# An output projection by seven block products (Strassen) instead of eight, in a hybrid decoder block

## Chip, cores, metric

The kernel runs on one core of a Trainium2 chip. The metric is the device time of one execution in microseconds (us). All arithmetic is float32: a product of two float32 matrices is made of three TensorE matmuls, since each operand is held as a rounded high part and a low remainder (hi·hi, lo·hi and hi·lo, summed in one PSUM bank).

## What is computed

One decoder block over 1024 tokens of width 1024: two branches (a state-space branch and a forgetting-attention branch, "fox") are gated and summed, and one projection takes the sum back into the residual stream. Cross-attention to 256 memory tokens and a gated feed-forward follow.

```python
D_MODEL = 1024; SEQ = 1024
out_a = glu_a * jax.nn.sigmoid(glu_b)            # state-space branch
out_b = att @ w_fox_o[l]                          # forgetting attention
gate_a, gate_b = jnp.split(jax.nn.sigmoid(gate_logits), 2, axis=-1)
h = h + (gate_a * out_a + gate_b * out_b) @ w_mix_out[l]      # <- the projection
h = h + memory_cross_attention(rms_norm(h, norm_mem_q[l]), ...)
f_a, f_b = jnp.split(rms_norm(h, norm_ffn[l]) @ w_ffn_in[l], 2, axis=-1)
h = h + (jax.nn.silu(f_a) * f_b) @ w_ffn_out[l]
```

## The kernel before

The kernel is written in stages. Within a stage a scheduler orders the instructions of each engine; each engine then runs its list in that order, and so do the queues of transfers (nearly all loads and stores are issued by SyncE, called SP; some stores by ScalarE). The part that the change touches is `stage_tail` and one place in the attention stage.

`fox_part(j)` makes rows 128j to 128j+127 of the gated sum, transposed (channels on partitions, tokens along the row), in two halves of 512 tokens: 12 matmuls for each half, times a gate that is loaded (`gb`), added to `sg`. The result is split at once into `mxh` (ScalarE cast) and `mxl` (VectorE subtraction) and stays in SBUF as `mT`. There are eight such parts, each 24 matmuls.

`mix(t, c, wm)` then makes 128 tokens times 512 output channels: eight blocks of 128 channels, three matmuls each, so 24 matmuls of 128x512 into one bank; a VectorE add puts the bank and a loaded piece of x (`xr`) into `H[t]`. Eight token tiles by two halves make 16 groups, 384 matmuls. The weights are loaded and split on chip (`whi`/`wlo` for c=0, `wbh`/`wbl` for c=1).

Two kinds of work are woven between those groups. `ahead(j)` splits the first feed-forward weights (`wpr` into `wph`, `wpl`) and stores them to `w_d`, by transfers that ScalarE issues. `norm(t)` normalises a finished tile for the memory attention: two squares on ScalarE (L190), small VectorE operations and a power on GpSimd (L207 to L217), one VectorE scaling into the single buffer `xs` (L231), eight TensorE transposes into two banks (L237), and a split into `u2h`, `u2l` (L183, L184). Tiles 0 to 3 are normalised behind groups 13 to 16 of the projection:

```python
    for t in range(4, NT):
        mix(t, 1, wm1)
        norm(t - 4, gq, u2)
```

`mem_q`, which follows, needs the normalised tiles 0 to 3 for its first matmul group. Much earlier, at the start of the attention stage, `Fox.run` copies the weights of the gated unit into `wg_d` by SP transfers, and then stores cumulated log-gates to `cum_d` (`cch`, `cl`) and loads them back as `hb`, which the first row-maximum matmul of the attention (L1763) reads.

Of the kernel before, what the change touches and what calls it, by code (L numbers as in the profile page):

```python
# [9 lines left out]
F32 = mybir.dt.float32  # L10
# [108 lines left out]
class Block:  # L119
# [125 lines left out]

    def norm_turn(self, xs, act, t):

        for b in range(2):
            cast = self.turned(self.turn(xs, b, ("misc", "pv")[b]), b, act, t)
        return cast  # L250
# [59 lines left out]
def hybrid_block_kernel(ctx: ExitStack, tc: tile.TileContext, x, mem, norm_mix, w_in, b_forget,  # L310
# [29 lines left out]
    sh = Shared(ctx.enter_context(tc.tile_pool(name="sh", bufs=1, reuse_waits="tile")))  # L340
    wg_d = B.dram.tile([4, P, 2 * D], F32, name="wg_d")
    glu = Glu(B, sh, yT, wg_d, gate_d)
    with tc.tile_pool(name="fox", bufs=1, reuse_waits="tile") as fp:
        fox = Fox(B, fp, sh, uT, w_in, b_forget[0], cum_d, rd_d, att_d)
        fox.run(y_d, yT, aT, w_glu, wg_d, [f for j in range(4) for f in glu.values(j)])
    glu.after = fox.maxima[NH - 2]
    with tc.tile_pool(name="st2", bufs=1, reuse_waits="tile") as s2:
        stage_tail(B, big, s2, sh, x, glu, aT, gate_d, kv_d, w_fox_o, w_mix_out, norm_mem_q[0], w_mem_q,
                   w_mem_o, norm_ffn[0], w_ffn_in, w_ffn_out, norm_final, out)
# [231 lines left out]

def stage_tail(B, big, s2, sh, x, glu, aT, gate_d, kv_d, w_fox_o, w_mix_out, g_mq, w_mem_q, w_mem_o, g_ffn,
               w_ffn_in, w_ffn_out, g_fin, out):
# [16 lines left out]

    mT = Act(s2, "t", NS2, 8, L, name="mx")
    fox = {}

    def fox_part(j):
# [6 lines left out]
        for h in range(2):  # L611
            cs = slice(512 * h, 512 * h + 512)
            po = B.bank(("pv", "pv", "misc")[(2 * j + h) % 3])
            B.gemm_t(po, fh[:, :, o:o + P], fl[:, :, o:o + P], aT, h, 4)
            gb = load(gate_d[D + j * P:D + (j + 1) * P, cs], "gb")
            V.tensor_mul(gb, gb, po)
            V.tensor_add(sg[:, cs], sg[:, cs], gb)
            mh, ml = mT.rhs(j, h)
            merged.append(B.split(mh, ml, sg[:, cs]))

    merged = []
    for j in range(8):
# [5 lines left out]
        if j > 2:  # L628
            fox_part(j - 3)
    for j in range(5, 8):  # L630
        fox_part(j)


    H = [bslot(name=f"h{t}") for t in range(NT)]
    gq = B.bcast_gain(s2, g_mq)
    u2 = Act(s2, "t", NS2, 8, L, name="u2")

# [4 lines left out]

    def wslots(src, pool_lo):

        nk = src.shape[0] // P
        raw = B.wpool.tile([P, RAW], F32, tag="raw", bufs=4, name="raw")[:, :D]
        S.dma_start(raw.rearrange("p (k c) -> p k c", k=nk), src.rearrange("(k p) c -> p k c", p=P))
        hl = bslot(F32R, "wbh"), bslot(F32R, "wbl")
        B.split(*hl, raw, pool_lo)
        return [t_.rearrange("p (k c) -> p k c", k=nk) for t_ in hl]  # L650

    def mix_weights(c):

        wm = ([], [])
        for kk in range(4):
            if c == 0:
                hl = B.wblock(w_mix_out, 2 * kk, 2, 0, 512)
            else:
                hl = wslots(w_mix_out[2 * kk * P:(2 * kk + 2) * P, 512:D], False)
            for w_, t_ in zip(wm, hl):  # L660
                w_ += [t_[:, 0, :], t_[:, 1, :]]
        return wm

    def mix(t, c, wm):
        cs = slice(512 * c, 512 * c + 512)
        ps = B.bank()
        gemm_n(ps, mT, t, wm, 8)
        V.tensor_add(H[t][:, cs], ps, load(x[t * P:(t + 1) * P, cs], "xr"))

    def norm(t, gb, act):  # L670
        xs = s2.tile([P, D], F32, tag="xs", bufs=1, name="xs")
        B.norm_scale(xs, H[t], B.rstd(H[t]), gb)
        return B.norm_turn(xs, act, t)

# [5 lines left out]
    def ahead(j):  # L680
# [14 lines left out]
        def plain():  # L695
            hl, _ = pair(0)
            with B.behind(merged[-1]):
                B.split(*hl, pre[j][0])
            for i, t_ in enumerate(hl):
                keep(i, t_)  # L700
# [34 lines left out]

    wm0 = mix_weights(0)
    with B.behind(merged[-1]):
        wm1 = mix_weights(1)
    mixes = [lambda t=t: mix(t, 0, wm0) for t in range(NT)] + [lambda t=t: mix(t, 1, wm1) for t in range(4)]
    weave(mixes, [f for j in range(AHEAD_IN + 1) for f in ahead(j)], 4)  # L740
    for t in range(4, NT):
        mix(t, 1, wm1)
        norm(t - 4, gq, u2)


    qT = Act(big, "big", 16, 4, L, name="mq")
# [260 lines left out]
    t_d = B.dram.tile([8, NP, P, 512], F32, name="t_d")  # L1007
    gs = {}

# [568 lines left out]
class Fox:  # L1578
# [279 lines left out]

    def run(self, y_d, yT, aT, w_glu, w_d, filler):
        B, fp, S = self.B, self.fp, self.B.S  # L1860
# [28 lines left out]
        with B.tc.issue_after(loaded.ins):  # L1889
            for k in range(4):  # L1890
                S.dma_start(w_d[k].rearrange("(m g) c -> m g c", g=8),
                            w_glu[k * P:(k + 1) * P].rearrange("(g m) c -> m g c", m=16))
        for f in pro[0].parts[:8] + pro[0].evac[:1] + pro[0].parts[8:] + pro[0].evac[1:]:
            f()
# [96 lines left out]
```

## Time and profile before

| | |
|---|---|
| three runs | 1541.27, 1540.81, 1539.42 us (median 1540.81) |
| span of the profiled execution | 1538.1 us (its own time outside the profiler isn't listed beside it) |
| TensorE (PE) busy | 1520.7 us, 99% |
| VectorE (DVE) busy | 1005.7 us, 65% |
| ScalarE (ACT) busy | 658.1 us, 43% |
| GpSimd (POOL) busy | 253.6 us, 16% |
| moved by transfers | 234.06 MB, mean 152 GB/s |

"Busy" is the time in which an engine has an instruction running; matmuls overlap, so their spacing, not their listed length, is what one costs. The median of the runs lies 2.7 us above the span. Times inside the span are counted from its start; the last part of the attention output and the projection lie between about 640 and 770 us.

### The profile page before, as it was taken

The page shows a single profiled execution, that of the slowest core. Times are in us where ns is not written, and L with a number is a line of the kernel's source. Part 1 is how long each engine was busy: PE and PEld are TensorE (multiplying, and loading weights), DVE is VectorE, ACT ScalarE, POOL GpSimd, SP SyncE. Part 2 cuts the span into 40 slices and gives each one's busy share as a digit, 9 for nine tenths or more (in the row PEclk, how much of TensorE's full clock was granted, in tenths as well). Part 3 has the DMA queues.
Part 4 walks back from the last instruction along what each step waited for, and adds up shares of the span by engine and source line. Part 5 has one row for each costly group of instructions (what it writes and reads, how often), then busy time and mean ns, then how long its engine had stood idle before and what let it go on. Part 6 is the DMA issues. An engine that isn't in the chain of part 4 may idle for free. (4 is left out here: it accounts for less than half of the span.)

```text
span 1538.1 us, 20434 instructions
## 1 busy us (share of the span) xinstructions
PE 1520.7 (99%) x7329; PEld 1257.7 (82%) x7329; DVE 1005.7 (65%) x1828; ACT 658.1 (43%) x1183; POOL 253.6 (16%) x341
## 2 busy tenths in 40 slices
PE   8999999999999999999999999999999999999998
PEld 7888888898777678888888888888888888888886
DVE  7936554355878867675556797777777775675555
ACT  7423334324667643232435663333333333354343
POOL 1166542100121214100102200000000000101001
PEclk9999999999999999999999999999999999999999
DMA  9634556611223746378210356555544544896542
GB/s 286 161 104 102 131 128 144 180 41 16 50 46 88 192 131 198 111 218 308 89 69 1 117 204 210 162 161 160 158 158 157 157 145 139 291 391 220 192 163 110
DMA packets 196293, 234.06 MB, mean 152 GB/s; under 512 B 35576, under 2 KB 127656, under 8 KB 195680
## 3 DMA queue, kind: packets, MB, share of 16 engines
q1 hardware_dynamic: 188704, 214.93, 47.0%
q10 hardware_dynamic: 7488, 17.83, 3.1%
q8 instruction: 57, 0.93, 0.3%
q14 instruction: 44, 0.36, 0.1%
HBM read 161.94 MB, written 72.71 MB: 153 GB/s over the span
## 5 line engine op out<-in xcount | busy, mean ns | idle before, releaser
L184 DVE TENSOR_TENSOR wlo<-raw,whi 128x1024 fp32r<-128x1024 f32 (+2 forms) x120 | 126.3, 1058 | 45.4 <-ACT whi L183 44.2
L183 ACT CAST whi<-raw 128x1024 fp32r<-128x1024 f32 (+2 forms) x120 | 108.7, 910 | 105.6 <-PE mm L174 39.1
L184 DVE TENSOR_TENSOR ol<-or,oh 128x1024 fp32r<-128x1024 f32 x73 | 90.1, 1236 | 74.0 <-ACT oh L183 71.9
L173 PE MATMUL mm<-uh,whi 128*128 128x512 f32 x344 | 136.5, 397 | 0.0
L174 PE MATMUL mm<-ul,whi 128*128 128x512 f32 x344 | 135.1, 393 | 0.0
L175 PE MATMUL mm<-uh,wlo 128*128 128x512 f32 x344 | 134.5, 391 | 0.0
L183 ACT CAST oh<-or 128x1024 fp32r<-128x1024 f32 x73 | 76.9, 1054 | 105.0 <-PE mm L1108 34.2
L997 POOL TENSOR_TENSOR g<-a,c 128x512 f32<-128x512 f32 x22 | 35.7, 1621 | 389.0 <-ACT a L996 389.0
L175 PEld LDWEIGHTS mm<-uh,wlo 128*128 128x128 f32 x344 | 64.7, 188 | 13.3 <-DVE wlo L184 0.2
L1803 POOL TENSOR_TENSOR pl<-pf,ph 128x512 fp32r<-128x512 f32 (+1 forms) x32 | 36.8, 1152 | 232.5 <-DVE ph L1802 193.3
L173 PEld LDWEIGHTS mm<-uh,whi 128*128 128x128 f32 x344 | 64.8, 188 | 11.6
L174 PEld LDWEIGHTS mm<-ul,whi 128*128 128x128 f32 x344 | 64.8, 188 | 11.0
L1800 ACT ACTIVATE pf<-sc 128x512 f32<-128x512 f32 (+1 forms) x96 | 46.4, 489 | 44.5 <-DVE sc L1796 28.3
L986 DVE SCALAR_TENSOR_TENSOR c<-c,pv 128x512 f32<-128x512 f32 x22 | 15.1, 687 | 76.5 <-ACT c L985 76.4
L211 POOL TENSOR_TENSOR r<-ms,mhalf 128x1 f32<-128x1 f32 (+1 forms) x26 | 15.7, 605 | 298.6 <-DVE ms L207 258.5
L964 PE MATMUL pv<-S3h,we 128*128 128x512 f32 x176 | 57.7, 389 | 0.0
L1806 DVE TENSOR_TENSOR pl<-pf,ph 128x512 fp32r<-128x512 f32 (+2 forms) x64 | 35.3, 553 | 10.4 <-ACT ph L1805 9.8
L1108 PE MATMUL mm<-ol,oh 128*128 128x512 f32 (+1 forms) x110 | 41.9, 381 | 0.0
L1108 PE MATMUL mm<-oh,ol 128*128 128x512 f32 (+1 forms) x110 | 41.9, 381 | 0.0
L1108 PE MATMUL mm<-oh 128*128 128x512 f32 (+1 forms) x110 | 41.9, 381 | 0.0
L173 PE MATMUL sc<-uh,whi 128*128 128x512 f32 x104 | 40.8, 392 | 0.0
L173 PE MATMUL mm<-yh,whi 128*128 128x512 f32 x104 | 40.7, 392 | 0.0
(639 smaller groups left out, 4554.2 us busy)
## 6 DMA issues: line engine op xcount, KB each, us to landing
or<-c_d SPq DMA_DIRECT2D x77, 256.0 KB
wo<-in_w_ffn_out_dram SPq DMA_DIRECT2D x22, 512.0 KB
c_d<-g SPq DMA_DIRECT2D x44, 256.0 KB
t_d<-wo SPq DMA_DIRECT2D x44, 256.0 KB
or<-t_d SPq DMA_DIRECT2D x44, 256.0 KB
rawb<-in_w_ffn_in_dram SPq DMA_DIRECT2D x20, 512.0 KB
raw<-in_w_ffn_in_dram SPq DMA_DIRECT2D x20, 512.0 KB
raw<-in_w_in_dram SPq DMA_DIRECT2D x19, 512.0 KB
```

What stands on the lines that cost most here:

```text
L173: T.matmul(ps, lh, rh, start=first, stop=False)
L174: T.matmul(ps, lh, rl, start=False, stop=False)
L175: return T.matmul(ps, ll, rh, start=False, stop=last)
L183: cast = self.A.copy(hi, src)
L184: self.rest = (self.G if pool_lo else self.V).tensor_sub(lo, src, f32(hi))
L211: self.G.tensor_tensor(out=r, in0=v, in1=self.mhalf[:, 0:n], op=ALU.pow)
L964: T.matmul(ps, l_[:, k, :], r_, start=first and k == 0 and i == 0, stop=k == 3 and i == 2, skip_group_check=True)
L997: G.tensor_mul(g[:, 512:], a1, c1)
L1108: T.matmul(ps, l_[:, gi], r_[:, c0:c1], start=k == 0 and (p == NP - LAST if own else p == 0 and n in (1, 2, 7)), stop=p == NP - 1 and k == ...
L1800: self.exp = A.activation(pf[:, off:], ps[:, off:], AF.Exp)
L1803: G.tensor_sub(pl[:, off:], pf[:, off:], f32(ph[:, off:]))
L1806: self.left = V.tensor_sub(pl[:, off:], pf[:, off:], f32(ph[:, off:]))
```

## The change

The 1024x1024x1024 product is cut into 2x2 blocks of 512 and made by seven block products of sums of blocks, numbered 1 to 7. The gated sum is no longer split and kept in SBUF: VectorE makes its sums of blocks in float32 (`merged_pair`, one for each pair of channel blocks) and SP stores them to `mc_d`, 28 pieces of 256 KB. The sums of the weight blocks are made by GpSimd (`mix_sums`, 16 additions of 128x512) and stored to `mt_d`, at the start of the attention stage, right behind the `wg_d` copies. For each of the 28 steps `m_get` loads the two operands side by side into one buffer, casts both in one ScalarE operation and makes the low parts on VectorE (left operand) and GpSimd (right operand). A step is 4 x 3 matmuls, 336 in all. `H` starts as x, loaded by transfers, and VectorE adds or subtracts a bank after each product (28 times, from PSUM). The last product but one runs tile by tile (`m_tile`), the last one, number 3, as four steps, and `norm(0)` to `norm(3)` are woven into these eight pieces, with both transposed halves in banks named "pv".

```diff
-    for j in range(5, 8):
-        fox_part(j)
...
+def mix_sums(B, w, mt_d, p):
+    w1, w2 = [B.wpool.tile([P, RAW], F32, tag="raw", bufs=4, name="wmix")[:, :D] for _ in range(2)]
+    for i, t_ in enumerate((w1, w2)):
+        B.S.dma_start(t_, w[(2 * p + i) * P:(2 * p + i + 1) * P, :])
+    b11, b12, b21, b22 = w1[:, :512], w1[:, 512:], w2[:, :512], w2[:, 512:]
+    for n, o, i in ((5, b11, b12), (7, b12, b22), (6, b22, b11), (4, b21, b22)):
+        B.G.tensor_add(o, o, i)
+        B.S.dma_start(mt_d[n, p], o)
...
+    def merged_pair(p):
+        ge, go = gs.pop(2 * p), gs.pop(2 * p + 1)
+        a21, a11, a22, a12 = ge[:, :512], ge[:, 512:], go[:, :512], go[:, 512:]
+        s24, s3 = slot(name="s24"), sh.half("s3")
+        for n, a_ in ((2, a12), (4, a22)):
+            S.dma_start(mc_d[n, p], a_)
+        V.tensor_sub(s3, a11, a21)
+        V.tensor_sub(a21, a22, a21)
...
+        for n, a_ in ((6, s24[:, :512]), (7, s3), (5, a21), (3, s24[:, 512:])):
+            S.dma_start(mc_d[n, p], a_)
...
+    MORDER = (1, 6, 7, 5, 4, 2, 3)
...
+    def m_get(m):
+        n, p = mseq[m]
+        r_ = B.wpool.tile([P, RAW], F32, tag="raw", bufs=4, name="raw")[:, :D]
+        S.dma_start(r_[:, :512], mc_d[n, p])
...
+        S.dma_start(r_[:, 512:], src)
...
+        A.copy(hl[0], r_)
+        V.tensor_sub(hl[1][:, :512], r_[:, :512], f32(hl[0][:, :512]))
+        G.tensor_sub(hl[1][:, 512:], r_[:, 512:], f32(hl[0][:, 512:]))
...
+    def m_step(m):
...
+        for i in range(4):
+            m_mm(m, i, set_[i])
+        if p == 3:
+            for i in range(4):
+                m_add(n, i, set_[i])
...
+    MAHEAD = 5
...
+    weave([lambda m=m: m_next(m) for m in range(2, 20)], [f for j in range(AHEAD_IN + 1) for f in ahead(j)], 4)
+    last = [lambda i=i: (m_tile(i), m_next(20 + i)) for i in range(4)] + [lambda m=m: m_step(m) for m in range(24, 28)]
+    weave(last, [lambda t=t: norm(t, gq, u2, ("pv", "pv")) for t in range(4)])
...
         for f in beside:
             f()
```

The order of instructions on the engines shows where this lands. Three places matter.

**The end of the projection, TensorE.** Before, the eight transposes of each of the four tiles (`xs` into misc and pv) stand between groups of 24 matmuls; this is the fourth set and what follows it:

```order
L173 MATMUL mm<-wbh,mxh_1_6008 128x512
L174 MATMUL mm<-wbl,mxh_1_6008 128x512
L175 MATMUL mm<-wbh,mxl_1_6016 128x512
L237 MATMUL misc<-ident,xs 128x128 x4
L237 MATMUL pv<-ident,xs 128x128 x4
L173 MATMUL sc<-u2h_0_6803,whi 128x512
L173 MATMUL mm<-u2h_0_6803,whi 128x512
```

Now the last rows of the projection (L693) and what follows; `moh` and `mol` are the split operands of a step:

```order
L693 MATMUL mm<-moh 128x512
L693 MATMUL mm<-mol,moh 128x512
L693 MATMUL mm<-moh,mol 128x512
L237 MATMUL pv<-ident,xs 128x128 x24
L173 MATMUL mm<-u2h_0_6722,whi 128x512
L174 MATMUL mm<-u2l_0_6730,whi 128x512
```

One set of eight transposes stands 22 matmuls ahead of the last product's end; the other three sets, 24 transposes, stand together behind the last matmul of the projection, directly before the first matmul of `mem_q`.

**The same place on VectorE.** Before, each tile's scaling stood one group of 24 matmuls behind the one before it:

```order
L668 TENSOR_TENSOR h_6798<-sc,xr 128x512
L184 TENSOR_TENSOR u2l_0_6811<-misc,u2h_0_6803 128x2x128
L231 SCALAR_TENSOR_TENSOR xs<-h_6795,r_7433,gbc 128x1024
L184 TENSOR_TENSOR u2l_0_6813<-misc,u2h_0_6805 128x2x128
L184 TENSOR_TENSOR u2l_0_6815<-pv,u2h_0_6807 128x2x128
```

Now (h_6714 to h_6721 are tiles 0 to 7; the adds L700 of h_6718 and h_6719 are those of the last product):

```order
L700 TENSOR_TENSOR h_6718<-h_6718,sc 128x512
L184 TENSOR_TENSOR u2l_0_6734<-pv,u2h_0_6726 128x2x128
L217 SCALAR_TENSOR_TENSOR r_7544<-rt_7545,r_7544 128x1
L215 TENSOR_TENSOR rt_7600<-r_7599 128x1
L700 TENSOR_TENSOR h_6719<-h_6719,sc 128x512
L231 SCALAR_TENSOR_TENSOR xs<-h_6715,r_7544,gbc 128x1024
L184 TENSOR_TENSOR u2l_0_6736<-pv,u2h_0_6728 128x2x128
L216 SCALAR_TENSOR_TENSOR rt_7600<-rt_7600,ms_7598 128x1
L700 TENSOR_TENSOR h_6720<-h_6720,mm 128x512
L217 SCALAR_TENSOR_TENSOR r_7599<-rt_7600,r_7599 128x1
L700 TENSOR_TENSOR h_6721<-h_6721,mm 128x512
```

The scaling of tile 1 stands behind the last product's second add, that of tile 2 behind its fourth, and tile 3's comes a further 16 rows later.

**SP at the start of the attention stage.** Before, nothing stands between the copies to `wg_d` and the cumulated gates:

```order
L1891 DMA wg_d<-in_w_glu_dram 128x1x2048 x3
L1663 DMA cum_d<-cch 8x1024
L1668 DMA cum_d<-cl 8x512 x2
L1701 DMA raw<-in_w_in_dram 128x8x64
L1702 DMA raw<-in_w_in_dram 128x8x64
L1741 DMA hb<-cum_d 2x1024
```

Now the transfers of `mix_sums` (24 in all) stand there; these are the last of them:

```order
L588 DMA wmix<-in_w_mix_out_dram 128x1024
L592 DMA mt_d<-wmix 128x512
L1740 DMA cum_d<-cch 8x1024
L592 DMA mt_d<-wmix 128x512 x3
L1745 DMA cum_d<-cl 8x512 x2
L1778 DMA raw<-in_w_in_dram 128x8x64
L1779 DMA raw<-in_w_in_dram 128x8x64
L1818 DMA hb<-cum_d 2x1024
```

The store of `cch` waits in SP's list for 13 of the 16 stores of weight sums, and `cl` and the loads of `hb` for all of them.

The same queue, later, where the products start. TensorE's list has three whole steps (36 matmuls) and parts 6 and 7 (48) mixed behind part 5, and then the fourth step. The left operand of that step is the first row below; its load is one of the x2:

```order
L633 DMA mc_d<-sg 128x512
L651 DMA mc_d<-s_6936 128x512
L644 DMA mc_d<-sg 128x512
L651 DMA mc_d<-sg 128x512
L670 DMA raw<-mc_d 128x512 x2
```

Between the store and the load stand three stores of `merged_pair(3)`, two of which need part 7's first half (`a22`, and `a22 - a21`).

More of the change, by code (lines that the diff above doesn't have):

```diff
@@ new lines, in m_mm, with m_add @@
+    def m_mm(m, i, ps):
+        n, p = mseq[m]
+        hi, lo = mops[m]
+        gi = slice(i * P, (i + 1) * P)
+        for k, (l_, r_) in enumerate(((hi, hi), (hi, lo), (lo, hi))):
+            T.matmul(ps, l_[:, gi], r_[:, 512:], start=k == 0 and p == 0 and n in (1, 2, 7),
+                     stop=p == 3 and k == 2, skip_group_check=True)
+    def m_add(n, i, ps):
+        t, c, op = {1: (4, 0, ALU.add), 2: (4, 0, ALU.add), 6: (0, 0, ALU.add), 7: (0, 1, ALU.subtract),
+                    5: (0, 1, ALU.subtract), 4: (0, 0, ALU.add), 3: (4, 1, ALU.subtract)}[n]
+        h = H[t + i][:, 512 * c:512 * c + 512]
+        return V.tensor_tensor(out=h, in0=h, in1=ps, op=op)
@@ L641, in gemm_n, with norm @@
             B.mm3(ps, ah, al, w[0][k], w[1][k], k == 0, k == nk - 1)
[L643 to L670, printed above, removed]
+    def norm(t, gb, act, banks=("misc", "pv")):
         xs = s2.tile([P, D], F32, tag="xs", bufs=1, name="xs")
         B.norm_scale(xs, H[t], B.rstd(H[t]), gb)
-        return B.norm_turn(xs, act, t)
+        return B.norm_turn(xs, act, t, banks)
     AHEAD_IN = 2
```

93 lines of the change are left out of this document (70 added, 23 removed).

## The prediction

> **What bounds the kernel now.** I read the page first, then TensorE's waits, then the busy time in the stretch of the projection.
>
> ```profile
> span 1538.1 us, 20434 instructions
> PE 1520.7 (99%) x7329; PEld 1257.7 (82%) x7329; DVE 1005.7 (65%) x1828; ACT 658.1 (43%) x1183; POOL 253.6 (16%) x341
> PE sc L258 <- POOL ident masks.py:199: 1.9, 1, 1.9
> PE mm L1763 <- DVE mc L1768: 1.2, 1, 1.2
> 680.00:700.00 20.00, 20.00 (x90) 16.53 (x89) 16.13 (x21) 8.74 (x12) 0.00 (x0) 1.00 0.91 283
> 700.00:720.00 20.00, 20.00 (x90) 16.57 (x89) 10.04 (x15) 4.51 (x7) 0.00 (x0) 1.00 0.79 269
> 720.00:740.00 20.00, 20.00 (x90) 16.57 (x89) 10.84 (x15) 7.92 (x13) 0.56 (x1) 1.00 0.91 328
> 1350.00:1370.00 20.00, 20.00 (x90) 16.57 (x89) 14.59 (x15) 10.49 (x11) 0.00 (x0) 1.00 1.05 393
> ```
>
> PE is busy 1520.7 of 1538.1 us. Its two longest waits of all are 1.9 and 1.2 us, and neither lies in the projection. In the rows of windows (stretch, its length, busy time and count of PE, its weight loads, DVE, ACT, POOL, then granted clock, busy share of the transfer engines, GB/s) PE is busy in the whole of the 60 us. So a matmul taken away there is worth its full spacing, and any microsecond in which PE waits is lost in full: nothing behind it has slack. The spacing comes from PE's timeline:
>
> ```profile
> 737.83 0.39 PE L174 MATMUL mm<-wbl,mxh 128*128 128x512 f32 x1
> 742.37 0.39 PE L173 MATMUL sc<-wbh,mxh 128*128 128x512 f32 x1
> ```
>
> These are 20 spacings apart: 4.54 / 20 = 0.227 us each.
>
> **Term 1, the matmuls.** 384 become 336: 48 x 0.227 = **-10.9 us**, all on PE.
>
> **Term 2, the end of the projection.** The order shows 24 transposes, those of tiles 1 to 3, behind the last product. One `xs` buffer makes the tiles a chain: scaling, transposes, cast, subtraction, next scaling. Before, the links look so:
>
> ```profile
> 734.40 1.22 DVE L184 TENSOR_TENSOR wlo<-raw,whi 128x1024 fp32r<-128x1024 f32 x1
> 735.53 0.21 DVE L207 TENSOR_SCALAR ms<-ss 128x1 f32<-128x1 f32 x1
> 736.41 0.16 DVE L215 TENSOR_TENSOR rt<-r 128x1 f32<-128x1 f32 x1 [0.67 <-POOL r L211]
> 750.30 0.39 PE L175 MATMUL mm<-wbh,mxl 128*128 128x512 f32 x1
> 750.53 0.60 PE L237 MATMUL misc<-ident,xs 128*128 128x128 f32 x4
> 750.73 0.69 DVE L668 TENSOR_TENSOR h<-mm,xr 128x512 f32<-128x512 f32 x1 [2.48 <-PE mm L175]
> 750.97 0.60 PE L237 MATMUL pv<-ident,xs 128*128 128x128 f32 x4
> 751.17 0.37 ACT L183 CAST u2h<-misc 128x256 fp32r<-128x256 f32 x1 [3.62 <-PE misc L237]
> 751.32 0.48 PE L173 MATMUL sc<-wbh,mxh 128*128 128x512 f32 x1
> 751.52 0.63 ACT L190 ACTIVATE junk<-h 128x512 bf16<-128x512 f32 x1
> 751.57 0.42 DVE L184 TENSOR_TENSOR u2l<-misc,u2h 128x256 fp32r<-128x256 f32 x1
> 751.91 1.28 DVE L231 SCALAR_TENSOR_TENSOR xs<-h,r,gbc 128x1024 f32<-128x1024 f32 x1
> 752.15 0.35 ACT L183 CAST u2h<-misc 128x256 fp32r<-128x256 f32 x1
> 752.40 0.63 ACT L190 ACTIVATE junk<-h 128x512 bf16<-128x512 f32 x1
> 770.63 0.19 PEld L173 LDWEIGHTS sc<-u2h,whi 128*128 128x128 f32 x1 [0.26 <-ACT u2h L183]
> ```
>
> A set of transposes takes 750.53 to 751.32 = 0.79 us. Before, PE ran a group of 24 matmuls (5.4 us) behind each set, which hid the chain; only 0.26 us was waited ahead of `mem_q` (last row). I follow the changed order of DVE and ACT with these durations, Z being the end of PE's last product. A square with its read-out keeps ACT from one cast to the next about 0.63 to 0.88 us (751.52 to 752.15, 752.40); I take 0.76.
>
> Tile 1: DVE ends the adds of the last product's first two tiles and the small operations between them at Z+0.7; the scaling, behind them in the list, ends about Z+2.0 to 2.3. Transposes to Z+3.2. ACT is in five squares (tiles 4 and 5 among them) and casts about Z+3.65 to 4.0, the second bank's after one more square at 5.1; DVE subtracts both first halves (0.34 apart) and scales tile 2: Z+5.5 to 6.8. Banks come free with the subtractions behind that, so its transposes run Z+7.1 to 8.3. Then DVE has `wlo` (1.22), four subtractions and eight small operations (0.2 each) ahead of tile 3's scaling: Z+11.5 to 12.8. Transposes to 13.6; the first matmul of `mem_q` at Z+13.85. Without the three sets (2.4) and the old wait (0.26) that is 11.2 us; `mem_q`'s next matmuls wait for the last casts, 0.4 more: **+11.6 us**. Bounds: if ACT and DVE did nothing else, a tile would take 1.28 + 0.04 + 0.79 + 0.37 + 0.42 = 2.9 us, the first scaling would end at Z+0.75 and the first matmul could start at Z+7.3: +4.9. At the other end, each link late by one more square or `wlo`: +14.
>
> **Term 3, the start of the products.** The fourth step's left operand goes out and comes back through DRAM behind stores that need part 7's first half.
>
> ```profile
> 598.13 1.92 SPq L597 DMA_DIRECT2D gb<-gate_d  x2
> 601.94 0.69 DVE L616 TENSOR_TENSOR gb<-gb,pv 128x512 f32<-128x512 f32 x1 [3.23 <-DMA gb<-gate_d]
> 602.66 0.69 DVE L617 TENSOR_TENSOR sg<-sg,gb 128x512 f32<-128x512 f32 x1
> 733.15 1.05 ACT L183 CAST whi<-raw 128x1024 fp32r<-128x1024 f32 x1 [0.71 <-DVE wpl L184]
> L1803 POOL TENSOR_TENSOR pl<-pf,ph 128x512 fp32r<-128x512 f32 x24 | 30.9, 1289 | 78.5 <-DVE ph L1802 73.0 <-DVE mboth L1776 5.6
> ```
>
> Count from the end of part 5. PE reaches the fourth step behind 31 + 48 + 5 = 84 matmuls: 19.1 us, and about 0.6 later because the first step's `mol` is late (cast 1.05, GpSimd subtraction 1.29 behind a load). Part 7's first half is done 12 matmuls before part 7's end, 67 x 0.227 = 15.2; DVE's product, sum and block sum (0.69 each, with one more between) end near 18.2; store issued, then the load; a 256 KB transfer takes about 2.2 us to its user (issued by 600.05 at the latest, where the pair's row ends; used 601.94; I add 0.3): 20.7. Cast 1.05: 21.8. PE waits 2.1; the low part on GpSimd adds 0.6 (not whole, since hi·hi goes first); the late first `mol` 0.6; and the change from product 1 to product 6, whose banks wait for four DVE adds with six other operations between them in the list, 0.6. Together **+3.9 us**, bounds 0 (all of it absorbed by reordering on other engines' idle time) and 6.
>
> **Term 4, the weight sums.** SP's list puts `cl` and `hb` behind all 16 stores.
>
> ```profile
> 293.73 9.79 SPq L1891 DMA_DIRECT2D wg_d<-in_w_glu_dram  x3
> 320.59 1.22 DVE L184 TENSOR_TENSOR wlo<-raw,whi 128x1024 fp32r<-128x1024 f32 x1 [1.63 <-ACT whi L183]
> 322.31 1.23 DVE L184 TENSOR_TENSOR wlo<-raw,whi 128x1024 fp32r<-128x1024 f32 x1
> 339.25 0.30 SPq L1663 DMA_DIRECT2D cum_d<-cch  x1
> 342.49 0.53 SPq L1742 DMA_DIRECT2D hb<-cum_d  x1
> 351.21 0.22 PE L1763 MATMUL pv<-hb 68*128 68x128 f32 x1
> L1252 POOL TENSOR_TENSOR sg<-sg,ga 128x512 f32<-128x512 f32 x16 | 25.7, 1628 | 77.0 <-DVE sg L1245 49.8 <-DMA ga<-gate_d 27.2
> ```
>
> Before, SP is idle from 303.5 to 339.25. The second pair's weights need buffers that `wlo` frees at 321.8 and 323.5. Behind a load (some 2.5 us) 12 additions of about 1.63 follow: 323.5 + 2.5 + 19.6 = 345.6, and hb, which before was loaded 3.2 us behind the first store to `cum_d`, lands near 350.5 to 353 where PE wants it at 351.2: **+1.0 us**, bounds 0 and 3. GpSimd itself has nothing to do then; PE's cover for the rest is the query projection that runs meanwhile.
>
> **Term 5, transfers.** In 680 to 740 the transfer engines are busy 0.91, 0.79 and 0.91 of the time: 52 us of 60. After, 28 steps load 14.7 MB instead of 4.2 MB of weights, and the last pair's stores are 1.8 MB: 12.3 MB more, at 393/1.05 = 374 GB/s some 33 us. With about 7 us from the 11 us before 680, that is 92 us of work in the 76 us between part 5's end and the last operands' loads. About 22 us of it are the stores to `w_d` (16 pieces of 512 KB, 8.4 MB), for which PE doesn't wait, and the operands are fetched five steps ahead (5 x 12 x 0.227 = 13.6 us). So most of the overload is hidden, but ACT casts operands and `wph` in one list, and a `wph` cast waits until an older store has freed its tile. I take **+2 us**, near the lower end; bounds 0 and 8 (the excess of 16, half of it borne by the stores).
>
> **Costed at nothing.** DVE loses 16 splits and gains 4 x 4 block sums and 28 left low parts; DVE is busy 37 of the 60 us in the windows above, and PE doesn't wait for the sums of pairs 0 to 2, made behind 24 matmuls each. The loads of x (16 pieces, now 8) are issued early.
>
> **Sum.** -10.9 + 11.6 + 3.9 + 1.0 + 2.0 = +7.6 us: the span 1538.1 becomes 1545.7. The runs' median stands 2.7 above the span, so 1540.8 + 7.6 = **1548.4 us**.
>
> **Rivals.**
> (a) *The end of the projection is hidden after all: faster.* If tiles 1 to 3 took what ACT and DVE need when undisturbed and the wait fell to the old 0.3, then -10.9 + 0.4 + 3.9 + 1 = -5.6, 1535. For it: tiles 0 to 3 are final 96 matmuls (21.8 us) before the end. Against it: the lists are fixed, and the three scalings stand behind adds that need the last product. It turns the sign when term 2 is below 3 us with term 5 at nothing; its own lower bound is 4.9.
> (b) *No change.* Term 2 at its lower bound and little at the start: -10.9 + 5 + 3.9 + 1 + 0 = -1, about 1540.
> (c) *Transfers bind.* Term 5 at 8: 1554.4. For it: the 92 us of work in 76; against it: the five steps of lead.
> (d) *The clock.* The first transposes of this trace ran slow after an idle start:
>
> ```profile
> 8.21 1.12 PE L237 MATMUL misc<-ident,xt 128*128 128x128 f32 x4 [0.88 <-DVE xt L231]
> 22.81 0.60 PE L237 MATMUL pv<-ident,xt 128*128 128x128 f32 x4
> ```
>
> Four took 1.12 us, later 0.60. Term 2 leaves PE idle for 3.9 and 4.5 us around a few transposes. If that slows it again, six half sets cost 0.5 more each on a chain (up to 3 us, less where the second half hides) and `mem_q` starts slow: +2 to +4, 1551. Against it: no idle time of this length inside the span before, so no row tells. The Trainium skill, "TensorE: Matmul & The Clock Gate", section "What's actually happening", says that the array falls to half clock after an idle window of about 3.4 us and needs about that much busy time to return; the first row agrees with a half-rate start, and by that rule rival (d) would hold.
>
> **Chances.** The sum as it stands 0.45 (its own range 1544 to 1552), (d) 0.20, (c) 0.13, (b) 0.14, (a) 0.08. About 0.2% (3.1 us) is what a measurement of this kernel can tell from no change, so same is 1537.7 to 1543.9. Faster 0.08, from (a); same 0.14, from (b); slower 0.78. The range from 1538.5 to 1556 leaves out (a) and the far end of (c) with (d).
>
> **What will show it.** Right: 336 L693 matmuls 0.227 apart; PE idle around the 24 transposes, with releases by `xs` (L231), some 11 us in all; a wait of 2 to 3 us at the fourth step for `moh`; a wait of about 1 us at the first row maximum for `hb`. Wrong: scalings of tiles 1 to 3 before the last product's end (term 2), no wait for `moh` (3), waits for `raw` loads from step 10 on (5 larger), transposes at 1.1 us for four (d). The likeliest way to be wrong is the size of term 2, since each link depends on what ACT happens to have ahead.

## The result, and the profile after

The changed kernel takes 1580.51 us (median of four runs, 1578.04 to 1583.12) against 1540.12 before: 2.6% slower, ratio 1.0261 with a 95% interval of 1.0246 to 1.0276. I had forecast 1548.4 (1538.5 to 1556). The sign was right, the loss five times as large: +40 us where +7.6 was forecast. One of the ten executions of e2, further down, took 6957.94 us for a reason that isn't known; without it e2's median is 1541.31 instead of 1541.58.

Top of the page, of the changed kernel:

```profile
span 1577.7 us, 20643 instructions
PE 1523.3 (97%) x7281; PEld 1255.9 (80%) x7281; DVE 1047.0 (66%) x1860; ACT 666.9 (42%) x1187; POOL 321.3 (20%) x385
...
DMA packets 208520, 260.30 MB, mean 165 GB/s; under 512 B 37048, under 2 KB 129128, under 8 KB 207904
```

PE has 48 matmuls less and still is busy 2.6 us longer than before: some of its work ran slower. Its waits (what waits, for what, us in all, times, longest):

```profile
PE mm L693 <- DVE h L700: 10.4, 1, 10.4
PE pv L1840 <- DMA hb<-cum_d: 6.4, 1, 6.4
PE sc L693 <- DVE mol L684: 4.0, 3, 2.2
PE pv L237 <- DVE rt L216: 3.7, 1, 3.7
PE pv L237 <- DVE u2l L184: 3.1, 1, 3.1
PE pv L237 <- DVE xs L231: 3.0, 2, 1.6
PE sc L693 <- ACT moh L683: 2.9, 1, 2.9
PE misc L1735 <- DVE logf L1722: 2.6, 1, 2.6
```

All but two of these lie in the projection; the two (6.4 and 2.6) are at the start of the attention stage. Five stretches show where PE ran at a lower granted clock (columns as in the prediction; the clock is the third number from the end):

```profile
350.00:380.00 30.00, 23.64 (x128) 20.70 (x128) 12.12 (x31) 7.01 (x13) 2.91 (x3) 0.83 0.42 65
680.00:700.00 20.00, 17.77 (x71) 14.15 (x70) 10.79 (x16) 3.05 (x3) 1.79 (x1) 0.91 0.94 333
700.00:720.00 20.00, 15.85 (x60) 11.96 (x59) 14.58 (x20) 6.59 (x7) 7.66 (x5) 0.91 0.83 288
760.00:780.00 20.00, 11.73 (x42) 9.51 (x43) 14.27 (x18) 4.11 (x7) 4.82 (x3) 0.74 0.84 281
800.00:820.00 20.00, 15.42 (x67) 12.94 (x68) 13.26 (x40) 7.23 (x21) 3.62 (x5) 0.74 0.09 27
```

Ten slow matmuls take 4.27 us (768.83 to 773.10, rows below), so they stand 0.427 us apart instead of 0.227: about half speed. A mean clock of 0.83 over 30 us is then 10 us at half speed, 0.91 over 20 us 3.6, and 0.74 over 20 us 10. Each of the five comes with a wait of PE, in it or just behind it.

For the comparison I use three landmarks of PE's timeline: the last matmul of the gated unit on `yh` and `whi`, the first of `mem_q` (on u2h), and the first of the feed-forward output (mm<-oh).

| kernel | last gated unit | projection, to mem_q | mem_q to ffn output |
|---|---|---|---|
| before | 657.4 | 113.2 | 563.4 |
| after | 668.2 | 139.9 | 565.3 |
| difference | +10.8 | +26.7 | +1.9 |

So 10.8 us are lost before the projection begins, 26.7 in it (although 10.9 us of matmuls are gone), and 1.9 behind it. I had forecast +1.0 for the first and +6.6 for the second (-10.9 + 11.6 + 3.9 + 2.0).

**The start of the attention stage.** SP, POOL and PE in the changed kernel:

```profile
300.53 22.38 SPq L588 DMA_DIRECT2D wmix<-in_w_mix_out_dram  x3
315.45 5.38 POOL L591 TENSOR_TENSOR wmix<-wmix 128x512 f32<-128x512 f32 x4 [22.29 <-DMA wmix<-in_w_mix_out_dram]
331.58 5.25 POOL L591 TENSOR_TENSOR wmix<-wmix 128x512 f32<-128x512 f32 x4 [3.42 <-DMA wmix<-in_w_mix_out_dram]
340.71 5.76 POOL L591 TENSOR_TENSOR wmix<-wmix 128x512 f32<-128x512 f32 x4 [3.88 <-DMA mt_d<-wmix]
346.87 0.33 SPq L1740 DMA_DIRECT2D cum_d<-cch  x1
349.03 4.03 POOL L591 TENSOR_TENSOR wmix<-wmix 128x512 f32<-128x512 f32 x3 [2.56 <-DMA mt_d<-wmix]
353.50 0.66 SPq L1745 DMA_DIRECT2D cum_d<-cl  x2
355.59 0.26 SPq L1818 DMA_DIRECT2D hb<-cum_d  x1
361.26 0.45 PE L1840 MATMUL pv<-hb 68*128 68x128 f32 x1 [6.36 <-DMA hb<-cum_d]
```

The additions come in groups, and between the last ones GpSimd stands 3.4, 3.9 and 2.6 us while its buffers are stored and loaded again. The last addition ended at 353.06 and the last store went out right behind it, and `hb` was issued 13 us later than before (355.90 against 342.49 for the same transfer). Meanwhile VectorE's log-gates ran slow. Groups of VectorE there, after and then before:

```profile
L1719 DVE SCALAR_TENSOR_TENSOR logf<-logf 128x64 f32<-128x64 f32 x7 | 5.3, 753 | 0.2
```

```profile
L1642 DVE SCALAR_TENSOR_TENSOR logf<-logf 128x64 f32<-128x64 f32 x7 | 1.6, 223 | 0.2
```

The same operation takes 753 ns instead of 223 while GpSimd adds beside it.

**In the projection.** The longest wait, with some rows of VectorE's list ahead of the add that ends it, a GpSimd operation beside them, and the first matmuls behind it:

```profile
754.77 0.68 DVE L785 TENSOR_TENSOR wpr<-wpr 128x512 f32<-128x512 f32 x1
754.94 3.37 POOL L685 TENSOR_TENSOR wlo<-raw,whi 128x512 fp32r<-128x512 f32 x2 [0.64 <-ACT whi L683]
755.37 1.79 DVE L684 TENSOR_TENSOR wlo<-raw,whi 128x512 fp32r<-128x512 f32 x1
757.08 1.77 DVE L786 TENSOR_TENSOR wpr<-wpr 128x512 f32<-128x512 f32 x1
767.45 0.68 DVE L700 TENSOR_TENSOR h<-h,mm 128x512 f32<-128x512 f32 x1
768.27 0.76 PE L693 MATMUL mm<-whi 128*128 128x512 f32 x1 [10.43 <-DVE h L700]
768.83 0.63 PE L693 MATMUL mm<-wlo,whi 128*128 128x512 f32 x1
773.10 0.47 PE L693 MATMUL mm<-whi,wlo 128*128 128x512 f32 x1
```

Product 4 ended at 757.7; its first add, which frees the bank mm for product 2, came at 767.45, behind 13 operations of VectorE from 753.65 on, eight of them sums and splits of the feed-forward weights. Beside a GpSimd operation that reads SBUF, a VectorE operation with both inputs in SBUF took 1.75 to 1.79 instead of 0.68; the adds L700, with one input in PSUM, took 0.68 everywhere. The Trainium skill, "SBUF — State Buffer", section "Who interferes with whom", says that a VectorE instruction with two SBUF inputs contends with a GpSimd instruction that reads SBUF, over a pair of ports that it calls an exclusive lock. The trace agrees, by the 1.1 us that these operations took longer. I had left that out of the prediction.

**The end of the projection.**

```profile
794.74 0.39 PE L693 MATMUL mm<-moh,mol 128*128 128x512 f32 x1
800.85 1.94 PE L237 MATMUL pv<-ident,xs 128*128 128x128 f32 x8 [3.06 <-DVE u2l L184]
806.52 1.94 PE L237 MATMUL pv<-ident,xs 128*128 128x128 f32 x8 [3.73 <-DVE rt L216]
808.11 0.78 PE L173 MATMUL mm<-u2h,whi 128*128 128x512 f32 x1
```

From the end of the last product (794.97) to the first matmul of `mem_q` are 13.1 us. The sets of eight transposes at 800.85 and 806.52 took 1.94 us each, listed, at the slow clock; the one at 796.72 took 1.06.

### The profile page after: what moved, and what is told of

It reads as the page before. It is cut to its first block, busy times and chain, and to the rows that moved or that the text cites. A ratio compares the mean times of both kernels' runs of the same rounds, so it can differ in the third digit from the quotient of the medians.

```text
span 1577.7 us, 20643 instructions
## 1 busy us (share of the span) xinstructions
PE 1523.3 (97%) x7281; PEld 1255.9 (80%) x7281; DVE 1047.0 (66%) x1860; ACT 666.9 (42%) x1187; POOL 321.3 (20%) x385
## 4 chain that ended last, share of the span: by engine, by line
PE 82%; DVE 7%; DMA 4%; ACT 3%; issue 2%; POOL 1%; SPq 0%; POOLq 0%; ACTq 0%; DVEq 0%
PE mm L1042 15%; PE pv L1042 8%; PE mm L173 7%; PE mm L175 7%; PE mm L174 7%; PE mm L1185 5%; PE sc L1042 4%; PE sc L1185 4%; PE pv L1185 3%; PE sc L173 3%; PE sc L175 3%; PE sc L174 3%; PE misc L1185 2%; PE sc L1870 1%; PE mm L1840 1%
## 5 line engine op out<-in xcount | busy, mean ns | idle before, releaser
L184 DVE TENSOR_TENSOR wlo<-raw,whi 128x1024 fp32r<-128x1024 f32 (+2 forms) x116 | 120.7, 1046 | 41.3 <-ACT whi L183 40.4
L183 ACT CAST whi<-raw 128x1024 fp32r<-128x1024 f32 (+2 forms) x116 | 104.6, 904 | 99.8 <-PE mm L174 38.2
L173 PEld LDWEIGHTS mm<-uh,whi 128*128 128x128 f32 x344 | 65.4, 190 | 11.6
L685 POOL TENSOR_TENSOR mol<-raw,moh 128x512 fp32r<-128x512 f32 x24 | 39.3, 1644 | 63.5 <-ACT moh L683 62.3
L683 ACT CAST moh<-raw 128x1024 fp32r<-128x1024 f32 x24 | 25.0, 1047 | 49.0 <-DMA raw<-mc_d 30.6
L1883 DVE TENSOR_TENSOR pl<-pf,ph 128x512 fp32r<-128x512 f32 (+2 forms) x64 | 35.3, 553 | 10.4 <-ACT ph L1882 9.7
```

The costliest lines, as they stand in the source:

```text
L173: T.matmul(ps, lh, rh, start=first, stop=False)
L183: cast = self.A.copy(hi, src)
L184: self.rest = (self.G if pool_lo else self.V).tensor_sub(lo, src, f32(hi))
L685: G.tensor_sub(hl[1][:, 512:], r_[:, 512:], f32(hl[0][:, 512:]))
L1883: self.left = V.tensor_sub(pl[:, off:], pf[:, off:], f32(ph[:, off:]))
```

## Experiments

The kernel before, run beside them, stood at 1540.0 to 1541.0 us; each difference is to it or to the changed kernel's 1580.5, as said. Where a kernel leaves something out, its expectation says what.

### The weight sums at the start of the attention stage

**e1**: the kernel before, with `mix_sums` added where the change has it.

```diff
+        for f in beside:      # mix_sums(p), p = 0..3, behind the copies to w_d
+            f()
```

> The kernel before with the weight sums of the change added at the start of the attention stage (loads, 16 GpSimd additions, 16 stores); nothing reads them and the projection is the old one. Theory A (the change's start of attention costs 10.8 us by itself: the list of SP holds the cumulated gates back, and the additions slow VectorE's small operations of the log-gates): 1540.1 + 10.8 = 1551, with a PE wait of about 6 us for hb and one of about 2.6 us for logf, and half a clock for 10 us behind them. Rival, the prediction's term 4: +1 us, 1541. Rival B (the delay comes only together with the new projection): no change.

Measured: 1550.57, ratio 1.0069 (1.0054 to 1.0084): +10.5 us. Its projection takes 113.2 us, as before. The waits:

```profile
PE pv L1776 <- DMA hb<-cum_d: 4.1, 1, 4.1
PE misc L1671 <- DVE logf L1658: 3.4, 1, 3.4
```

So the loss at the start comes from the sums alone, and doesn't depend on the projection.

**e2**: e1 without the additions.

```diff
-        B.G.tensor_add(o, o, i)
```

> As the run above, but without the 16 GpSimd additions: the same loads and the same 16 stores, of unsummed blocks. If the additions are the cause (their chain of buffers and the slowed VectorE), the stores are done by about 335, before the cumulated gates are ready at 339, and the time is 1540 to 1542. If the places in SP's list and the transfers are the cause, most of the 10.8 us stays: 1546 to 1551.

Measured: 1541.58, ratio 1.0010 (1.0000 to 1.0019). PE waits 1.1 us for `hb`. Eight loads and 16 stores at the same place in SP's list cost at most 2 to 3 us; the rest comes with the additions, through the stores that wait for them or through the slower VectorE.

**e2b**: e1 with the additions on VectorE.

```diff
-        B.G.tensor_add(o, o, i)
+        B.V.tensor_add(o, o, i)
```

> The kernel before with the weight sums alone, as in the first experiment (+10.5 us with GpSimd), but with the 16 additions on VectorE at the same place. Theory (GpSimd's 1.3 us for each addition in a chain of buffers, and VectorE's two-operand operations held up meanwhile): an addition takes 0.6 us and holds up nothing, the last store goes out some 6 to 9 us earlier, and the time is 1541 to 1543. Rival (the chain of buffers and the place in SP's list cost the time whatever the engine): 1547 to 1551.

Measured: 1564.80, ratio 1.0159 (1.0144 to 1.0175). Both theories missed: it is 14 us worse than on GpSimd. The log-gates ran at their old speed, but the scheduler put the additions behind them in VectorE's list, and SP's list stood still until they came:

```profile
PE pv L1776 <- DMA hb<-cum_d: 22.9, 1, 22.9
345.71 3.47 DVE L591 TENSOR_TENSOR wmix<-wmix 128x512 f32<-128x512 f32 x5
367.45 0.35 SPq L1676 DMA_DIRECT2D cum_d<-cch  x1
```

`cch` went out 28 us later than before (339.25). So the loss doesn't need GpSimd's hold on VectorE. In e1 and e2b PE waits for `hb`, which stands in SP's list behind stores that wait for additions. The direct test, the sums behind `hb` in that list, was not run.

**e11**: e2b in five other buffers, written ahead of the copies to `wg_d` (the edit of the buffers is shown).

```diff
-    w1, w2 = [B.wpool.tile([P, RAW], F32, tag="raw", ...
+    w1, w2 = [sh.tmp("wmix") for _ in range(2)]
```

> The kernel before with the weight sums alone, on VectorE, in five buffers that are free at that time instead of the four that the projections of the attention use, and written ahead of the copies to wg_d. If the delay is one of the buffers and the list, all of it goes: 1540 to 1541.5. If loads and stores of 8 MB at this place cost by themselves: 1543 or more.

Measured: 1558.42, ratio 1.0121 (1.0106 to 1.0136). Missed again: the buffers were free, but the stores again waited for late additions, and `cch` went out behind 13 of them at 359.18. The time lies where transfers that cost by themselves were expected (1543 or more), but e2 shows them to cost little.

**e15**: the changed kernel with the sums in the gated-unit stage, still on GpSimd.

```diff
+        if j in (3, 4, 5, 6):
+            mix_sums(B, w_mix_out, mt_d, j - 3)
```

> The changed kernel with only the weight sums moved (still on GpSimd) from the start of the attention stage to the gated-unit stage, woven with its parts 3 to 6, where no cumulated gates stand behind them in SP's list. If the place in SP's list is the cause of the 10.5 us: -8 to -11, 1570 to 1572. If the additions and 8 MB of transfers cost PE something wherever they stand: 1575 or more.

Measured: 1592.64, 12 us slower than the changed kernel. The wait at the start of the attention is gone, and another takes its place in the gated unit:

```profile
PE mm L173 <- DVE sg L1318: 17.6, 1, 17.6
```

There the gate products on GpSimd and the loads of the gates and of the unit's weights stand in the same two lists. The place at the start was not the worst one: in both places what stands in SP's list behind stores that wait for additions came late.

### The projection

**e3**: the changed kernel with the right operands' low parts on VectorE.

```diff
-        G.tensor_sub(hl[1][:, 512:], r_[:, 512:], f32(hl[0][:, 512:]))
+        V.tensor_sub(hl[1][:, 512:], r_[:, 512:], f32(hl[0][:, 512:]))
```

> The changed kernel with the right operand's low part made on VectorE instead of GpSimd (28 subtractions of 128x512 move). Theory (a GpSimd operation holds up a VectorE subtraction of two SBUF operands for its whole length, 0.68 becomes 1.75 us): VectorE gets 28 x 0.6 = 17 us more work but loses about 1.1 us of waiting on each of some 20 operations; the wait of 10.4 us for the adds shrinks by 2 to 3 us: 1577, range 1573 to 1581. Rival (the longer times of VectorE are due to something else, and the GpSimd subtractions run for free beside it): VectorE falls further behind and the time rises by 8 us or more, 1589.

Measured: 1579.57, against 1580.51 the same. VectorE's group of these operations, in the changed kernel and then in e3:

```profile
L684 DVE TENSOR_TENSOR mol<-raw,moh 128x512 fp32r<-128x512 f32 x24 | 21.9, 916 | 9.8 <-ACT moh L683 9.8
```

```profile
L684 DVE TENSOR_TENSOR mol<-raw,moh 128x512 fp32r<-128x512 f32 x24 | 16.4, 685 | 5.9 <-ACT moh L683 5.9
L685 DVE TENSOR_TENSOR mol<-raw,moh 128x512 fp32r<-128x512 f32 x24 | 16.4, 683 | 0.0
```

The hold is real, since 916 ns became 685 without a GpSimd operation beside it; but the 28 subtractions more cost VectorE what the hold had cost: it was busy 1045.8 us in all, against 1047.0. GpSimd's help was worth nothing here, and cost nothing.

**e4**: product 2 in the sc banks.

```diff
-        ps = B.bank(("mm", "misc")[i % 2])
+        ps = B.bank("sc")
```

> The changed kernel with the last product but one in the two sc banks, which product 5 left long before, instead of mm and misc, which wait for product 4's adds. If the bank alone is the cause of the wait of 10.4 us: -10 us and its slow clock (2.5) too, 1568. If VectorE's list, which is full until 786, sets the end, the wait moves to the following products and tiles: -2 to -5, 1576 to 1578.

Measured: 1582.84, outside both expectations and no gain. The wait for the add is gone, and PE waits longer for operands:

```profile
PE sc L693 <- ACT moh L683: 16.8, 3, 7.6
```

**e7**: e4, and norms 0 to 3 written ahead of product 3.

```diff
+    for i in range(4):
+        m_tile(i)
+        m_next(20 + i)
+        norm(i, gq, u2, ("misc", "pv"))
```

> The changed kernel with product 2 in the sc banks and with norm(0) to norm(3) written one behind each tile of product 2, ahead of product 3; the order of the engines then has the transposes at 266 to 300 of the 336 matmuls instead of at the end. If the end of the projection was a chain that the order made (prediction's term 2): its four waits of 9.8 us and the slow clock around them go, -10 to -14, 1567 to 1571. If VectorE and the transfers are behind whatever the order: the waits move forward to the operands of product 3, and the gain is under 5 us.

Measured: 1580.14, no gain. From the last product to `mem_q` there is no wait left; the projection takes 140.7 us instead of 139.9, with waits of 6.8 and 8.4 us for operands at 763 and 782. So the order of the norms made the chain at the end, but taking the chain away gained nothing while the preparation was in the projection: other waits took its place.

**e13**: products 1 and 7 take pairs 0 to 2 first.

```diff
+    mseq[:12] = [(n, p) for n in (1, 7) for p in range(3)] + [(1, 3), (7, 3)] + [(6, p) for p in range(4)]
```

> The changed kernel with only the order of the first steps changed: products 1 and 7 take pairs 0 to 2 first, six steps, and then pair 3, so that the operand that comes back through DRAM behind part 7 is needed 36 matmuls (8.2 us) later. If the waits at 706 and 708 (3.8 us and the slow clock behind them) are that chain (prediction's term 3): -4 to -6, 1575 to 1577. If the products are bound by transfers or VectorE further on, the gain is lost again at the adds of product 4: within 2 us of 1580.5.

Measured: 1585.58, 5 us slower. The wait for pair 3 shrinks from 3.8 to 1.8 us; a wait of 3.7 for product 1's adds appears, and the chain of norms at the end waits 12.0 us instead of 8.4.

**e5**: the preparation of the feed-forward weights moved to the memory attention.

```diff
-    weave([... m_next(m) for m in range(2, 20)], [f for j in range(AHEAD_IN + 1) for f in ahead(j)], 4)
+    for m in range(2, 20): m_next(m)
...
+    for f in [f for j in range(AHEAD_IN + 1) for f in ahead(j)]: f()      # behind cross(0)
```

> The changed kernel with the preparation of the feed-forward weights (loads, splits, sums, stores to w_d) moved out of the projection to the start of the memory attention. The projection costs 28.6 us more than before in the changed kernel. Theory B (in the projection the work of VectorE, ScalarE and the transfers together no longer fits under 336 matmuls, and PE waits for operands and for adds): most of the 28 us of waits and their slow clock go, -20 to -30 us, 1550 to 1560, if the memory attention has room for the moved work. Rival C (the waits come from the chain through DRAM and the chain of norms alone): only the tail changes, -5 to -10, 1571 to 1576.

Measured: 1589.62, against the theory as a whole. But the projection takes 113.2 us instead of 139.9: its 26.7 us are gone. They come back, and more, behind it (600.5 us from `mem_q` to the feed-forward output instead of 565.3), where the pieces stand in a block. With the preparation out, the scheduler also puts the norms early, as in e7; since e7 alone took 140.7 us, the order isn't what made the difference. So what lengthened the projection is the preparation sharing it with the new work; and with it out, the 10.9 us saved are still taken by 7.3 us of waits and the slow clock behind them.

**e9** and **e10** part the preparation into its transfers and its arithmetic.

```diff
 e9 (keep)
+            if (j, n) == (0, 0):
                 A.dma_start(w_d[j, n], f32(t_))
 e10 (plain, sums, seventh, rest)
-            B.split(*hl, pre[j][0])
+            keep(0, pre[j][0]); keep(1, pre[j][-1])
```

> The changed kernel without 15 of the 16 stores to w_d (7.9 MB less in the projection; the feed-forward part reads the one stored piece each time instead, so its weights are not those of the reference). VectorE and ScalarE still do the splits and sums. If transfers bind the projection (prediction's term 5): operands land earlier, and the time falls by 10 us or more, to 1570 or less. If VectorE's list binds: little, -5 at most from the shorter tail that the order now shows, 1575 to 1580.

> The changed kernel with all loads and all 16 stores of the feed-forward preparation, but without its splits and sums on ScalarE and VectorE (the loaded pieces are stored as they are, so the weights used later are not those of the reference). If VectorE's list binds: the wait of 10.4 us for the adds goes and the tail shortens, -20 us, 1560. If transfers bind: operands still come late, and only -5 to -10, 1571 to 1576.

Measured: 1566.25 without the stores, 1575.29 without the arithmetic; projections of 128.4 and 137.6 us. In both, the scheduler also puts the norms early, as in e7, so e7's 140.7 us (with product 2 in the sc banks besides) is the nearest to compare with: the stores are worth 12 us, the arithmetic 3. By what was expected of them, both runs speak for the stores. Two stretches, of e9 and then of e10:

```profile
740.00:760.00 20.00, 16.74 (x74) 13.51 (x72) 19.93 (x25) 10.32 (x13) 11.07 (x7) 1.00 0.63 211
```

```profile
700.00:720.00 20.00, 12.67 (x47) 9.60 (x46) 8.74 (x13) 2.09 (x2) 3.03 (x2) 0.77 1.02 347
```

In e9 the transfer engines have room (0.63) and VectorE is busy in 19.93 of 20 us, with a wait of 10.7 for the adds still there. In e10 VectorE has room and the transfer engines have none (1.02, as the stores now go out early), with waits of 7.1 and 3.0 us for operands. So VectorE's list and the transfers each hold PE up when the other is relieved; 12 and 3 us are together 15 of the 27.5 between e7 and e5, and the rest went only where both were out.

What the stores do isn't settled by e9, because they stand in ScalarE's list, which also casts the operands. In the changed kernel a cast stood behind a store that waited for VectorE:

```profile
717.11 0.33 ACTq L762 DMA_DIRECT2D w_d<-wpl  x1
717.61 1.05 ACT L683 CAST moh<-raw 128x1024 fp32r<-128x1024 f32 x1 [6.07 <-DVE wpl L184]
```

From 680 to 800 ScalarE's idle time ahead of operand casts that `wpl` released is 11.3 us in e7 and none in e9. So e9's 12 us can come from room for the transfers, from a freed list of ScalarE, or both. The stores issued by another engine would tell; that was not run.

### Can it win?

**e14**: e11's sums, e13, e7, and the preparation woven with norms 4 to 7. **e16**: the sums as in e15, and the preparation held behind norm 3. **e17**: e16 with e3's edit.

```diff
 e16
+    def held(f):
+        with B.behind(n3):          # n3: the last cast of norm(3)
+            f()
```

> All edits together: weight sums on VectorE in free buffers ahead of wg_d (removes the 10.5 us), products 1 and 7 first, product 2 in the sc banks, norms 0 to 3 ahead of product 3, and the preparation of the feed-forward weights moved into the first half of the memory queries, woven with norms 4 to 7. If the causes add up as read from the traces (start of attention 10.8, waits and slow clock of the projection 28.6 + 10.9): the projection comes out at or below the old one and only the moved preparation costs, 1538 to 1550. If the preparation has no room in the memory attention, as when it stood behind it: 1555 to 1565.

> As the run with all edits (1568.5), but with the weight sums on GpSimd in the gated-unit stage, and with the preparation of the feed-forward weights held behind the split of norm 3, so that the scheduler can't draw it back into the projection. Theory (VectorE's list in the projection is too full with the preparation in it, and the sums cost only where gates stand behind them): sums -17, and the wait of 5.3 us for xs at 770 and its slow clock go: 1541 to 1549; it may reach the old kernel's 1540.5 but not beat it by more than 3. Rival (the preparation costs as much in the memory attention as in the projection): 1552 to 1560.

> As the run before, with the right operands' low parts on VectorE instead of GpSimd. With room in VectorE's list, freeing it of the 1.1 us it is held up beside each GpSimd subtraction should weigh about as much as the 0.6 us of each moved one: within 3 us of the run before. If GpSimd's hold is what delays operands and adds: 3 to 6 us faster than it.

Measured: 1568.45, 1577.47 and 1580.01; e14 and e16 came out slower than both of their ranges, so these edits don't add up as expected. By landmarks e14 loses 17.8 us at the start (e11 alone: +17.6 in time), 4.4 in the projection and 6.9 behind it; e16 loses 23.2, 1.4 and 13.0. e17 is 2.5 us off e16, within what was expected of no effect.

**e18** leaves both costs out, **e19** adds the edits of e7 and e13.

```diff
-        B.G.tensor_add(o, o, i)
...
-        return [fetch, plain, sums, seventh, rest] if j < AHEAD_IN else [first, plain]
+        return [first, kept_]         # one load, one store, for j = 0 only
```

> The changed kernel without the 16 additions of weight blocks (the blocks are stored unsummed) and without the preparation of the feed-forward weights but for one load and one store of a piece that the feed-forward part then reads each time: neither output nor weights are those of the reference. What is left in the projection is the seven products with their operands. If the two costs found (10.5 us of the sums in SP's list, an overfull list of VectorE and of transfers in the projection) are the whole loss: the wait of 10.4 us for product 4's adds and the tail's 9.8 go; what stays is the start's waits (5 to 8 us) and the clock behind them (3) against the 10.9 us saved: 1537 to 1543. If the chains through DRAM or the norms cost by themselves: 1550 or more.

> As the run before, with products 1 and 7 first, product 2 in the sc banks and norms 0 to 3 ahead of product 3. If the start's waits are then the only loss left: 3 to 6 us faster than the run before, 1532 to 1538, the most that seven products could bring here. If the order of the first steps only shifts the wait to the adds of products 1 and 7, as when it was tried alone: within 2 us of the run before.

Measured: 1547.62 (ratio 1.0044, 1.0029 to 1.0059) and 1546.69 (1.0038, 1.0024 to 1.0052). Both are still slower than the old kernel, though that one does the whole preparation. e18 lies between its two ranges, and e19 within 2 us of e18, as expected if the new order only shifts the wait. The projection alone takes 118.9 and 117.1 us against 113.2. That e18 takes longer than e5's 113.2, with no preparation in either, isn't explained; its waits are 10.1 us against 7.3. The waits of e19:

```profile
PE sc L693 <- DVE mol L684: 4.0, 1, 4.0
PE misc L237 <- DVE xs L231: 2.2, 1, 2.2
PE sc L693 <- ACT moh L683: 1.3, 1, 1.3
```

Waits of 10.7 us in all remain in its projection, as much as the 48 matmuls saved: for the first steps' operands (4.0, 1.3, 0.9), for a norm (2.2) and some below one. Which edit would take these away was not tried, nor how the remaining 3.9 us over the old stage divides; so these runs show that seven products didn't win here, not that they can't.

## Why the prediction was wrong

- **Term 1**, -10.9 us: right. 336 matmuls, 0.227 us apart where PE doesn't wait and its clock is full.
- **Term 2**, the end of the projection, +11.6: right as a place and in size. Forecast Z+13.85 to the first matmul of `mem_q`, measured 13.1. But it was no cost that stands by itself: e7 took the chain away and the time stayed. So the right size bears out the chain, not the sum.
- **Term 3**, the start of the products, +3.9 (0 to 6): low. PE waited 2.2, 2.9, 0.9, 0.3 and 1.5 us there (683 to 723), 7.9 in all, and ran at half clock twice for 3.6 us, which costs 1.8 each. At 706, the wait for the fourth step's operand (2.9) and its low part (0.9), 3.8, is what I had worked out as 2.1 and 0.6.
- **Term 4**, the weight sums, +1.0 (0 to 3): wrong, +10.5 by e1. I had 12 additions of 1.63 us back to back behind one load of 2.5, for which I had no row, and the last one at 345.6. The additions took only 1.3, but the buffers had to be stored and loaded again: the load issued at 325.37 was used at 331.58, 6.2 us later, GpSimd stood 3.9 and 2.6 us more ahead of the next groups, and the last addition ended at 353.1. And I took `hb` as landed 2 us behind its issue where it took 5.7. The clock then halved for 10 us, which I hadn't counted there. (The first pair's load took 15 us, 300.53 to 315.45, behind the copies to `wg_d`; its additions were still done at 320.8, ahead of the buffers that the next pair needed.)
- **Term 5**, transfers, +2 (0 to 8), and **"costed at nothing"** for VectorE: the step that failed most. I compared VectorE's busy time before (37 of 60 us) with its own gains and losses as sums over the stage, took the transfers apart from it, and counted the stores to `w_d` as hidden since PE doesn't wait for them. The wait of 10.4 us for product 4's adds, with 2.4 of slow clock behind it, is in no term: the add stood behind 13 operations of VectorE. The stores were worth 12 us (e9), and with the preparation elsewhere all of the 26.7 us were gone (e5), or all but 5.7 (e18). So the helpers' work did not fit behind 336 matmuls; how the loss divides between VectorE's list, ScalarE's list and the transfers stays open. GpSimd's hold on VectorE is in the traces, but e3 shows that doing without GpSimd gains nothing.
- **Rival (a)**: by my own sum, with term 5 at nothing, the sign turns when term 2 is below 6.0, not 3; at 3 the gain would be as large as the 3.1 us that can be told from no change.
- **Rival (d)**, the clock, came true beside the others: the 28.1 us of waits (19.7 up to the last product, 8.4 behind it) less 10.9 make 17.2 of the 26.7; of the 9.5 left the slow clock adds about 7.8, as an estimate from the rows above (12 matmuls of 0.2 more from 768.27, two sets of transposes of 0.9 more, 1.8 each behind 684 and 708). The other 1.7 is about what the ten waits leave out, since a wait is counted from a matmul's listed end (0.39) and not from its spacing (0.227). The Trainium skill, "TensorE: Matmul & The Clock Gate", section "What's actually happening", gives half speed after an idle window of some 3.4 us and a like time of work to return; the trace agrees in half speed (0.427 against 0.227, about 1.9 times) and in waits of that order, and differs in that waits of 2.2 us, and of 2.9 with 0.9 behind it, were enough.

What I would do with the same profile: count the share of each helper resource in the stage after the change (VectorE's list, transfers), at the durations beside the other engines, and ask of each in-order list what stands behind an item whose data come from another engine.

## What to carry to other kernels

A saving on a busy engine is worth its full time only while every helper behind it still fits: here 10.9 us of matmuls were bought with 26 MB of transfers (234 to 260) and some 40 us of VectorE (1005.7 to 1047.0), in a stage whose transfer engines had been busy 0.79 to 0.91 of the time. Before such a change, find out what already sits in the shadow of the stage; it is what will surface. And a store in an in-order list that waits for another engine's result held up what stood behind it, in SP's list and in ScalarE's. To put such a store behind what is urgent, or in a list of its own, is the edit to try; no run here tried just that.

## What was unexpected of the hardware

A VectorE subtraction of two SBUF operands took 1.75 to 1.79 us instead of 0.68 beside a GpSimd subtraction, and a 128x64 operation 753 ns instead of 223; operations with a PSUM input didn't change (0.68). PE's clock fell to half with waits of 2 to 3 us, for some 3.6 us, and for about 10 us in the stretches of the long ones; the wait of 10.4 us cost 2.4 more by 12 slow matmuls behind it.
